# Hybrid decoder trunk, one core: the second product's first weights loaded ahead of two weight blocks, one PSUM bank changed, table steps and convolution taps put elsewhere

## The chip, the cores and the metric

The kernel runs on one core of one Trainium2 chip. Times are device microseconds (us) of a whole execution; "before" is the median of three runs. The trace is one further execution, taken by the hardware profiler. Engine names are the profile's: PE is TensorE's matmul, PEld its weight load, DVE is VectorE, ACT is ScalarE, POOL is GpSimd, SP is SyncE, which here only issues DMAs.

## The reference, cut to what matters

A sequence of 512 tokens of width 1024, all in float32, goes through two layers. The first is a recurrent layer, the second an attention layer, and each ends in a SwiGLU unit with 2816 hidden columns.

```python
def causal_depthwise_conv(x, w, b):            # 4 taps per channel
    y = lax.conv_general_dilated(x, w[:, None, :], ..., feature_group_count=x.shape[-1])
    return y + b

def recurrent_mixer(h, w_in, conv_w, conv_b, ga_w, ga_b, gx_w, gx_b, lam, w_out):
    y_branch, x_branch = jnp.split(h @ w_in, 2, axis=-1)
    gate = jax.nn.gelu(y_branch, approximate=True)
    xc = causal_depthwise_conv(x_branch, conv_w, conv_b)
    return (gate * rg_lru(xc, ga_w, ga_b, gx_w, gx_b, lam)) @ w_out

def swiglu(h, w_in, w_out):
    g, u = jnp.split(h @ w_in, 2, axis=-1)
    return (jax.nn.silu(g) * u) @ w_out

h = h + recurrent_mixer(rms_norm(h, ...), ...);          h = h + swiglu(rms_norm(h, ...), ...)   # layer 1
h = h + dilated_attention_mixer(rms_norm(h, ...), ...);  h = h + swiglu(rms_norm(h, ...), ...)   # layer 2
```

`rg_lru` multiplies blocks of 128 channels of the convolved branch with two gate matrices. The attention uses tables of cosines and sines of the positions (rotary embedding).

## The kernel before, in words

**Matmuls.** Every float32 product is made of three matmuls over a high part (h) and a low part (l) of each operand: `mm3`, lines 163 to 165. So each weight piece that arrives raw by DMA has to be split first: ACT casts it to the high part (L117, or L656 for the SwiGLU's first product), and DVE subtracts that from the raw piece to get the low part (L124, L657). A piece is 128 x 1024. The class `Stream` loads raw pieces into two buffers named wr, by SP's DMA queue, and splits them into three pairs named wh and wl.

**Order.** In most of the program a scheduler orders the instructions of each engine by dependencies and priorities. Inside a SwiGLU (`swiglu`), DVE, ACT, SP, POOL and PE run in exactly the order in which the code is written. SP takes its DMAs in that order too, and an issue that waits holds up all behind it.

**The recurrent layer's projection** goes over 16 blocks of 128 output columns; the first eight are the x branch. For each block `x_block` evicts the PSUM bank with a DVE multiply into xp (L443 for block 4, at high priority; L445 for the others), makes the first tap of the convolution on ACT (blocks 0 to 3, L449) or POOL (blocks 4 to 7, L451), and the other three taps on DVE (L453). `x_parts` splits the result into xch and xcl (L279, L280), and `x_gates` multiplies these with the gate matrices; its second product of each block uses the two banks tagged PT, one of which block 4 of the projection holds at first.

**A SwiGLU** starts with four plain blocks (`plain_block`, weights wr). Then the hidden columns go in five groups q = 0 to 4 (`ORDERS`), each as seven products named GA, GB, S1 to S4 and UB, which share operands in the manner of Strassen and Winograd: S1 and S3 are sums of weight blocks, made by a plain DMA on SP and an accumulating DMA on POOL (`fetch`, L640 and L642). "O" in the list is an out block, a part of the second product (`out_block`); in group 0 it makes four outputs b = 0 to 3, evicted by L776 into the residual h, in later groups two, evicted by L774. "L" splits the operands of the next out blocks (`parts_of`, L729 and L730).

```python
MIDDLE = "S1.T1 GA.B11 GB.B21 L S2.T2 O O S3.T3 O S4.B22 O UB.T4"
ORDERS = ["GA.B11 GB.B21 O S1.T1 S2.T2 O S3.T3 S4.B22 UB.T4", MIDDLE, MIDDLE, MIDDLE,
          "S1.T1 GA.B11 GB.B21 L S2.T2 O S3.T3 S4.B22 UB.T4 O O L O"]
```

So the step numbers s are 0 to 3 for the plain blocks and 4 to 12 for group 0; the first out block is step 6, between GB and S1. Each product has two outputs in two banks. GA uses the two banks PT; GB uses X and one of the three mm; S1 uses O and S. After GB, DVE adds its two banks to GA's result (`gate`, L700), which frees X and the mm bank; the plain blocks and the out blocks take mm banks in turn, and the out block's third output (b = 2) takes S in step 6 and X in step 9.

**Tables.** The rotary tables (`rotary`, L875 to L929, small DVE operations and two Sin activations) are a generator. The first SwiGLU advances it by one `yield` after step 9 and after each step from 13 on.

**Attention** stands between the two SwiGLUs and isn't touched.

Of the kernel before, what the change touches and what calls it, by code (L numbers as in the profile page):

```python
# [20 lines left out]
ALU = mybir.AluOpType  # L21
# [3 lines left out]
T = 512  # L25
# [28 lines left out]
def behind(tc, inst, f):  # L54

    tc.add_manual_dep(inst.ins, f.ins.name, mybir.DependencyInfo(
        mybir.DependencyClass.NoSync, mybir.DependencyReason.DATA), reason="order")
# [99 lines left out]
def trunk(tc, A, out):  # L157
    nc = tc.nc
    V, S, G, PE = nc.vector, nc.scalar, nc.gpsimd, nc.tensor

    def mm3(ps, w, x, first, last, on=False):
        (wh, wl), (xh, xl) = w, x
        PE.matmul(ps, wh, xh, start=first, stop=False, skip_group_check=on)  # L163
        PE.matmul(ps, wh, xl, start=False, stop=False, skip_group_check=on)  # L164
        PE.matmul(ps, wl, xh, start=False, stop=last, skip_group_check=on)  # L165
# [55 lines left out]
    with tc.tile_pool(name="keep", bufs=1) as kp, tc.tile_pool(name="wts", bufs=3) as wp, \  # L221
# [6 lines left out]
        def bank(tag=None, name="ps"):  # L228
            tag = tag or next(rotation)
            return pp.tile([128, 512], F32, name=name, tag=tag, bufs={"mm": 3, "PT": 2}.get(tag, 1))  # L230
# [42 lines left out]
        def split(src, gain, hi, lo):  # L273
            a = S.activation(hi, src, AF.Copy, scale=gain)  # L274
            V.scalar_tensor_tensor(lo, src, gain, hi.bitcast(F32), ALU.mult, ALU.subtract)
            return a
# [13 lines left out]
        def gain(c, k):  # L290
            return par[:, c + k:c + k + 1]
# [46 lines left out]
        with tc.tile_pool(name="lru", bufs=2) as lp, \  # L338
# [32 lines left out]
            for k in range(KB):  # L371
                with tc.high_priority():
                    a = split(h[k], gain(C_AN, k), xh[k], xl[k])
# [5 lines left out]
            def in_block(i, tag=None, between=None, at=5):  # L379
                ps = bank(tag)  # L380
                wh, wl = ws.get(i)
                for k in range(KB):
                    c = slice(128 * k, 128 * k + 128)
                    mm3(ps, (wh[:, c], wl[:, c]), (xh[k], xl[k]), k == 0, k == KB - 1)
                    if k == at and between:
                        between()
                return ps

            parts = [ws.get(0), ws.get(1)]
            first = [bank(), bank()]  # L390
# [15 lines left out]
            rb = norm[1]  # L406
# [10 lines left out]
            def perm(t):  # L417
                return t.rearrange("q (n i p) -> q n p i", n=4, i=32, p=4)

            def mine(t):  # L420
                return t.rearrange("q (n p i) -> q n p i", n=4, p=4, i=32)
# [16 lines left out]
            def x_block(b, ps):  # L438
                xp = lp.tile([128, 640], F32, name="xp", bufs=2)[:, :T + 4]
                G.memset(xp[:, 0:3], 0.0)  # L440
                if b == 4:
                    with tc.high_priority():
                        V.tensor_tensor(perm(xp[:, 3:3 + T]), mine(ps), mine(rb), ALU.mult)  # L443
                else:
                    V.tensor_tensor(perm(xp[:, 3:3 + T]), mine(ps), mine(rb), ALU.mult)  # L445
                xc = lp.tile([128, T], F32, name="xc", bufs=5)
                cw = [par[:, C_CW + 4 * b + j:C_CW + 4 * b + j + 1] for j in range(4)]
                if b < 4:
                    S.activation(xc, xp[:, 0:T], AF.Identity, bias=gain(C_CB, b), scale=cw[0])  # L449
                else:  # L450
                    G.tensor_scalar(xc, xp[:, 0:T], cw[0], gain(C_CB, b), ALU.mult, ALU.add)  # L451
                for j in range(1, 4):
                    V.scalar_tensor_tensor(xc, xp[:, j:j + T], cw[j], xc, ALU.mult, ALU.add)  # L453
                return b, xc

            def x_parts(b, xc):
# [50 lines left out]
                hgl[b] = lp.tile([128, T], F32R, name="hgl", tag=f"gated{b}", bufs=1)  # L507
                halve(z, hgh[b], hgl[b])

            xs, ys, decayed, ready = [], [], [], 0  # L510
            ws.asp = 2
            for i, m in enumerate(lru_order):
                ps = first.pop(0) if first else in_block(p_in + i)

                if i in (5, 6, 8, 9):
                    for _ in range(2):
                        b = xs[0][0]
# [23 lines left out]
            for ms in ((0, 1), *((m,) for m in range(2, 8))):  # L541
                parts = [ws.get(p_aout + m) for m in ms]
                first = [bank() for m in ms]
# [8 lines left out]
        def by_time(t):  # L552
            return t.rearrange("q (t a i) -> q a t i", t=4, a=4)

        def in_turn(t):
            return t.rearrange("q (a t i) -> q a t i", t=4, a=4)
# [11 lines left out]
        def swiglu(fp, p, after, meanwhile=iter(())):  # L568
# [64 lines left out]
            def fetch(q, n):  # L633
                if q == len(ORDERS):
                    return
                r = raws[q, n] = fp.tile([128, 4, 512], F32, name=n, bufs=1)
                u, k = {"GA": (0, 0), "GB": (0, 1), "S1": (1, 0), "S3": (0, 0), "UB": (1, 1)}[n]
                for i in range(2):
                    c = r[:, 2 * i:2 * i + 2]
                    nc.sync.dma_start(c, p.part(u, q, k, i))  # L640
                    if n in ("S1", "S3"):
                        nc.gpsimd.dma_start(c, p.part(1, q, n == "S1", i), accum_op=ALU.add)  # L642
# [120 lines left out]
            def out_block(c, m, i):  # L763
                nb = 2 if c else 4
                wh, wl = (t.rearrange("q (b k m) -> q b k m", b=nb, m=128) for t in ws.get(i))
                nk = 8 // nb
                src = [x if c else x[:, 2:4] for x in chunks[c]]
                for b in range(nb):
                    ps = bank("mm" if b != 2 else "X" if m else "S")
                    for k in range(nk):  # L770
                        mm3(ps, (wh[:, b, k], wl[:, b, k]), [x[:, k] for x in src], k == 0, k == nk - 1)
                    x = h[m + b]
                    if c:
                        V.tensor_tensor(by_time(x), by_time(x), in_turn(ps), ALU.subtract)  # L774
                    else:
                        V.tensor_tensor(x, x, ps, ALU.subtract)  # L776
# [4 lines left out]
            with tc.manual_schedule(engines={E.PE, E.DVE, E.Activation, E.SP, E.Pool}):  # L781
                ws.load_to(p.steps[2][3])
                fetch(0, "GA")
                ws.load_to(p.steps[3][3])
                for n in ("GB", "S1", "S3", "UB"):
                    fetch(0, n)
                for s, (kind, *what) in enumerate(p.steps):
                    if kind == "product" and what[0] == len(ORDERS) - 1:
                        ws.al = 4
                    {"plain": plain_block, "product": product, "out": out_block, "parts": parts_of}[kind](*what)  # L790
                    early.get(s, lambda: None)()
                    if s == 9 or s > 12:
                        next(meanwhile, None)
                for _ in meanwhile:
                    pass
# [13 lines left out]
        with tc.tile_pool(name="tables", bufs=1) as rp:  # L809
            rp = Pool(rp)  # L810
            with tc.tile_pool(name="ffn1", bufs=2) as fp:
                fp = Pool(fp)
                tables = []

                def make_tables():
                    tables.extend((yield from rotary(nc, A, rp, fp)))

                def after_f1(m, ps):
                    V.tensor_tensor(by_time(h[m]), by_time(h[m]), in_turn(ps), ALU.subtract)
                    split(h[m], gain(C_KV, m), xh[m], xl[m])  # L820
                    squares(m, Temps(fp))

                swiglu(fp, p_f1, after_f1, make_tables())


            with tc.tile_pool(name="att", bufs=2) as ap:
                ap = Pool(ap)
                attention(tc, A, ap, ws, dict(locals()))

        with tc.tile_pool(name="ffn2", bufs=2) as fp:  # L830
            fp = Pool(fp)

            def after_f2(m, ps):

                halves = [(slice(0, 2), nc.scalar), (slice(2, 4), nc.sync)]
                for c, queue in halves if m == 7 else [(slice(0, 4), nc.sync)]:
                    x = by_time(h[m])[:, :, c]
                    V.tensor_tensor(x, x, in_turn(ps)[:, :, c], ALU.subtract)
                    c = slice(128 * c.start, 128 * c.stop)
                    queue.dma_start(out[m][:, c], h[m][:, c])  # L840

            swiglu(fp, p_f2, after_f2)
# [532 lines left out]
```

## Time and profile before

| | |
|---|---|
| median of three runs | 1179.7 us (1177.21 to 1182.56) |
| the profiled execution | 1177.11 us |
| its span, from the first to the last instruction | 1175.1 us |
| granted TensorE clock | 1.00 throughout |
| PE busy | 1153.3 us, 98% of the span |
| DVE busy | 852.3 us, 73% |
| ACT busy | 623.3 us, 53% |
| POOL busy | 189.1 us, 16% |
| moved by DMA | 179.61 MB, mean 153 GB/s |
| first SwiGLU, first matmul of group 0's GA | 175.5 us of the span |
| second SwiGLU, last matmul of group 0's GB | 861.1 us |

A row of the order of time gives the start in us, the duration in us, the engine, the line, the operation, the tiles (out<-in; buffer numbers left out, so S stands for S1 and S3, wr for all raw buffers), the shapes, how many instructions of the kind are merged in it (x4), and in brackets how long the engine stood idle before it and whose end let it go. A row of waits gives the total in us, the number of waits and the longest. TensorE's matmuls overlap: one lasts 0.39 us but the next starts 0.23 us after it.

### The profile page before, as it was taken

What the parts mean: (1) busy time and instruction counts of PE and PEld (TensorE: products, weight loads), DVE (VectorE), ACT (ScalarE), POOL (GpSimd) and SP (SyncE); (2) the same over time, 40 slices, a digit from 0 to 9 for tenths busy, and PEclk for the clock granted to TensorE, in tenths of its full rate; (3) what the DMA queues carried; (4) which work ended last, traced back from release to release, by engine and by line L of the source; (5) the groups of instructions that cost most, each with busy time, mean ns of one, the idle gap of its engine ahead of it and who ended that gap; (6) DMA issues with size and microseconds to landing.
All of it is one profiled execution on the core that took longest, in us unless ns stands there. A gap on an engine that the chain in (4) does not pass through costs nothing.

```text
span 1175.1 us, 15129 instructions
## 1 busy us (share of the span) xinstructions
PE 1153.3 (98%) x5403; PEld 951.6 (81%) x5403; DVE 852.3 (73%) x1525; ACT 623.3 (53%) x901; POOL 189.1 (16%) x221
## 2 busy tenths in 40 slices
PE   9999999999999999999999999999989999999998
PEld 6787887878888888888888888898868888888887
DVE  8988687877767676887564677765968767676764
ACT  6796455543535353665555677655545535353532
POOL 4210010201001000010511334341101101001000
PEclk9999999999999999999999999999999999999999
DMA  7643365965665722433988658435648675757324
GB/s 238 155 112 108 108 225 151 236 182 162 182 170 166 193 73 81 132 101 99 222 178 179 136 120 178 108 73 126 227 115 231 182 177 165 193 160 181 89 65 133
DMA packets 92234, 179.61 MB, mean 153 GB/s; under 512 B 8704, under 2 KB 27008, under 8 KB 92160
## 3 DMA queue, kind: packets, MB, share of 16 engines
q1 hardware_dynamic: 72720, 130.80, 34.7%
q0 software_dynamic: 18864, 47.19, 22.8%
q8 instruction: 43, 0.70, 0.3%
q10 hardware_dynamic: 576, 0.66, 0.2%
q14 instruction: 31, 0.25, 0.1%
HBM read 164.99 MB, written 2.10 MB: 142 GB/s over the span
## 4 chain that ended last, share of the span: by engine, by line
PE 82%; DVE 6%; DMA 4%; issue 3%; ACT 2%; POOL 1%; SPq 0%; ACTq 0%; DVEq 0%; POOLq 0%
PE ps L165 22%; PE ps L164 22%; PE ps L163 21%; PE ps L1038 5%; PE ps L1039 5%; PE ps L1040 5%; DMA wr<-in_f_out 2%; DVE xc L453 1%; PE ps L1117 1%; PE ps L1204 1%; DMA wl<-in_w_in 1%; DMA GB<-in_f_in 1%; ACT pr L1190 0%; DMA h<-in_x 0%; DVE xp L445 0%
## 5 line engine op out<-in xcount | busy, mean ns | idle before, releaser
L117 ACT CAST wh<-wr 128x1024 fp32r<-128x1024 f32 (+2 forms) x136 | 131.1, 969 | 141.3 <-PE ps L164 80.9
L164 PE MATMUL ps<-wl,xh 128*128 128x512 f32 x320 | 124.6, 389 | 0.0
L165 PE MATMUL ps<-wh,xl 128*128 128x512 f32 x320 | 124.6, 389 | 0.0
L163 PE MATMUL ps<-wh,xh 128*128 128x512 f32 x320 | 124.6, 389 | 0.0
L165 PE MATMUL ps<-gh,wl 128*128 128x512 f32 x288 | 114.7, 398 | 1.9 <-DVE wl L124 1.7
L124 DVE TENSOR_TENSOR wl<-wr,wh 128x1024 fp32r<-128x1024 f32 (+2 forms) x93 | 100.0, 1084 | 21.9 <-ACT wh L117 21.5
L163 PE MATMUL ps<-gh,wh 128*128 128x512 f32 x288 | 113.8, 395 | 1.7 <-ACT wh L117 1.7
L164 PE MATMUL ps<-gl,wh 128*128 128x512 f32 x288 | 113.6, 395 | 0.0
L642 POOL DMA_DIRECT2D S<-in_f_in x40 | 48.2, 1248 | 380.9 <-DMA S<-in_f_in 241.3
L656 ACT CAST wh<-S 128x1024 fp32r<-128x1024 f32 x60 | 63.0, 1050 | 76.1 <-PE ps L165 33.8
L163 PE MATMUL ps<-xh,wh 128*128 128x512 f32 x256 | 101.0, 396 | 0.6 <-ACT xh L274 0.6
L165 PE MATMUL ps<-xh,wl 128*128 128x512 f32 x256 | 100.0, 391 | 0.7 <-DMA wl<-in_w_in 0.7
L164 PE MATMUL ps<-xl,wh 128*128 128x512 f32 x256 | 100.2, 391 | 0.1
L163 PE MATMUL ps<-wh,T 128*128 128x512 f32 x240 | 93.8, 391 | 5.4 <-DVE h L776 5.4
L657 DVE TENSOR_TENSOR wl<-S,wh 128x1024 fp32r<-128x1024 f32 x60 | 73.2, 1223 | 33.6 <-ACT wh L656 33.6
L165 PE MATMUL ps<-wh,T 128*128 128x512 f32 x240 | 93.5, 390 | 0.0
L164 PE MATMUL ps<-wl,T 128*128 128x512 f32 x240 | 93.5, 389 | 0.0
L1038 PE MATMUL ps<-wh,xh 128*128 128x512 f32 x224 | 91.5, 408 | 0.0
L1040 PE MATMUL ps<-wh,xl 128*128 128x512 f32 x224 | 87.7, 392 | 0.0
L1039 PE MATMUL ps<-wl,xh 128*128 128x512 f32 x224 | 87.4, 390 | 0.0
L774 DVE TENSOR_TENSOR h<-h,ps 128x512 f32<-128x512 f32 x64 | 43.4, 686 | 55.6 <-PE ps L165 55.4
L163 PEld LDWEIGHTS ps<-wh,xh 128*128 128x128 f32 x320 | 60.1, 188 | 12.7
(285 smaller groups left out, 2673.5 us busy)
## 6 DMA issues: line engine op xcount, KB each, us to landing
S<-in_f_in SPq DMA_DIRECT2D x40, 512.0 KB, 6.4
S<-in_f_in POOLq DMA_DIRECT2D x40, 512.0 KB, 8.9
wr<-in_f_out SPq DMA_DIRECT2D x36, 512.0 KB, 5.3
wr<-in_w_q SPq DMA_DIRECT2D x28, 512.0 KB, 6.8
wl<-in_w_q POOLq DMA_DIRECT2D x28, 512.0 KB, 7.6
GA<-in_f_in SPq DMA_DIRECT2D x20, 512.0 KB, 4.8
GB<-in_f_in SPq DMA_DIRECT2D x20, 512.0 KB, 7.5
UB<-in_f_in SPq DMA_DIRECT2D x20, 512.0 KB, 5.6
```

The lines of the kernel that those rows point to most:

```text
L117: nc.scalar.copy(hi[:, c], r[:, c])
L124: a = eng.tensor_tensor(lo[:, c], r[:, c], hi[:, c].bitcast(F32), ALU.subtract)
L163: PE.matmul(ps, wh, xh, start=first, stop=False, skip_group_check=on)
L164: PE.matmul(ps, wh, xl, start=False, stop=False, skip_group_check=on)
L165: PE.matmul(ps, wl, xh, start=False, stop=last, skip_group_check=on)
L642: nc.gpsimd.dma_start(c, p.part(1, q, n == "S1", i), accum_op=ALU.add)
L656: S.copy(hi, r)
L657: V.tensor_tensor(lo, r, hi.bitcast(F32), ALU.subtract)
L774: V.tensor_tensor(by_time(x), by_time(x), in_turn(ps), ALU.subtract)
L1038: PE.matmul(ps[t], xh[k][:, r], wh[:, c], start=k == 0, stop=False)
L1039: PE.matmul(ps[t], xh[k][:, r], wl[:, c], start=False, stop=False)
L1040: PE.matmul(ps[t], xl[k][:, r], wh[:, c], start=False, stop=k == 7)
```

## The change: what it does

There are four edits, in `x_block` and in `swiglu`.

1. **Weights of the second product.** The transfers of S3 and UB for group 0 are issued after step 0 instead of before it. The raw weights of the first out block are requested within step 0, so on SP's queue they now stand ahead of S3 and UB. This holds for both SwiGLUs.
2. **A bank.** The third output of the first out block (step 6, m = 0, b = 2) takes bank X instead of S.
3. **The tables' steps.** After step 12 the generator is advanced only after out blocks and after the products S3 and S4.
4. **The convolution.** Block 3's three DVE taps are put off until block 4's bank has been evicted, and the first of them is ordered behind that eviction; block 4's eviction loses its high priority.

```diff
-                if b == 4:
-                    with tc.high_priority():
-                        V.tensor_tensor(perm(xp[:, 3:3 + T]), mine(ps), mine(rb), ALU.mult)
-                else:
-                    V.tensor_tensor(perm(xp[:, 3:3 + T]), mine(ps), mine(rb), ALU.mult)
+                out_of_bank = V.tensor_tensor(perm(xp[:, 3:3 + T]), mine(ps), mine(rb), ALU.mult)
...
-                for j in range(1, 4):
-                    V.scalar_tensor_tensor(xc, xp[:, j:j + T], cw[j], xc, ALU.mult, ALU.add)
+
+                def taps(first=None):
+                    for j in range(1, 4):
+                        a = V.scalar_tensor_tensor(xc, xp[:, j:j + T], cw[j], xc, ALU.mult, ALU.add)
+                        if first and j == 1:
+                            behind(tc, a, first)
+
+                if b == 4:
+                    put_off.pop()(out_of_bank)
+                if b == 3:
+                    put_off.append(taps)
+                else:
+                    taps()
                 return b, xc
...
-                    ps = bank("mm" if b != 2 else "X" if m else "S")
+                    ps = bank("X" if b == 2 else "mm")
...
-                for n in ("GB", "S1", "S3", "UB"):
+                for n in ("GB", "S1"):
                     fetch(0, n)
...
                     early.get(s, lambda: None)()
-                    if s == 9 or s > 12:
+                    if s == 0:
+                        fetch(0, "S3")
+                        fetch(0, "UB")
+                    if s == 9 or s > 12 and (kind == "out" or kind == "product" and what[1][:2] in ("S3", "S4")):
                         next(meanwhile, None)
```

The bank changes no engine's order, only what an instruction waits for. The other edits move instructions at these places.

SP's queue at the start of the second SwiGLU before; wr175 is the fourth plain block's piece, wr180 and wr185 are the weights of the two out blocks of group 0:

```order
L640 DMA GA_7595<-in_f2_in 128x2x512 x2
L100 DMA wr175_7598<-in_f2_in 128x1024
L640 DMA GB_7600<-in_f2_in 128x2x512 x2
L640 DMA S1_7603<-in_f2_in 128x2x512 x2
L640 DMA S3_7608<-in_f2_in 128x2x512 x2
L640 DMA UB_7613<-in_f2_in 128x2x512 x2
L93 DMA wr180_7617<-in_f2_out 128x4x256
L93 DMA wr185_7810<-in_f2_out 128x4x256
```

and with the change (lines 640 and 642 are now 647 and 649):

```order
L647 DMA GA_7595<-in_f2_in 128x2x512 x2
L100 DMA wr175_7598<-in_f2_in 128x1024
L647 DMA GB_7600<-in_f2_in 128x2x512 x2
L647 DMA S1_7603<-in_f2_in 128x2x512 x2
L93 DMA wr180_7609<-in_f2_out 128x4x256
L647 DMA S3_7682<-in_f2_in 128x2x512 x2
L647 DMA UB_7687<-in_f2_in 128x2x512 x2
L93 DMA wr185_7810<-in_f2_out 128x4x256
```

The first out block's weights have moved ahead of S3's and UB's four transfers; the rest stands as before.

DVE in the convolution before, from the evictions of blocks 2 and 3 on; xp_432 and xc_435 belong to block 2, xp_440 and xc_443 to block 3, xp_456 and xc_459 to block 4, xp_528 to block 5:

```order
L445 TENSOR_TENSOR xp_432<-ps_262,rb_345 128x4x4x32
L445 TENSOR_TENSOR xp_440<-ps_310,rb_345 128x4x4x32
L453 SCALAR_TENSOR_TENSOR xc_435<-xp_432,par_74,xc_435 128x512
L453 SCALAR_TENSOR_TENSOR xc_443<-xp_440,par_74,xc_443 128x512
L453 SCALAR_TENSOR_TENSOR xc_435<-xp_432,par_74,xc_435 128x512
L453 SCALAR_TENSOR_TENSOR xc_443<-xp_440,par_74,xc_443 128x512
L453 SCALAR_TENSOR_TENSOR xc_435<-xp_432,par_74,xc_435 128x512
L453 SCALAR_TENSOR_TENSOR xc_443<-xp_440,par_74,xc_443 128x512
L443 TENSOR_TENSOR xp_456<-ps_356,rb_345 128x4x4x32
L445 TENSOR_TENSOR xp_528<-ps_464,rb_345 128x4x4x32
L280 TENSOR_TENSOR xcl_537<-xc_435,xch_536 128x512
L453 SCALAR_TENSOR_TENSOR xc_459<-xp_456,par_74,xc_459 128x512
```

and with the change (L441 is the eviction of every block, L451 the taps on DVE; block 4's tiles are now xp_453 and xc_456, and xcl_541 is block 3's low part):

```order
L441 TENSOR_TENSOR xp_440<-ps_310,rb_345 128x4x4x32
L451 SCALAR_TENSOR_TENSOR xc_435<-xp_432,par_74,xc_435 128x512 x3
L441 TENSOR_TENSOR xp_453<-ps_356,rb_345 128x4x4x32
L451 SCALAR_TENSOR_TENSOR xc_443<-xp_440,par_74,xc_443 128x512
L280 TENSOR_TENSOR xcl_537<-xc_435,xch_536 128x512
L451 SCALAR_TENSOR_TENSOR xc_443<-xp_440,par_74,xc_443 128x512
L451 SCALAR_TENSOR_TENSOR xc_456<-xp_453,par_74,xc_456 128x512
L451 SCALAR_TENSOR_TENSOR xc_443<-xp_440,par_74,xc_443 128x512
L451 SCALAR_TENSOR_TENSOR xc_456<-xp_453,par_74,xc_456 128x512
L483 TENSOR_TENSOR gated0_408<-ig_511,xc_419 128x512
L280 TENSOR_TENSOR xcl_541<-xc_443,xch_540 128x512
```

Block 4's eviction now stands behind three taps instead of six, block 5's has moved to a later place, and block 3's low part stands behind two taps of block 4. On PE the gate product that takes over block 4's bank stands eight matmuls of the projection earlier than before.

DVE in group 1 of the first SwiGLU before; L700 is the gate after GB, L730 the operands of the out blocks, wl52 and wl53 the low parts of their weights:

```order
L700 TENSOR_TENSOR e_2089<-ps_2093,e_2089 128x512
L875 TENSOR_SCALAR grow_1855<-grow_1855 128x384
L876 CAST posf_1861<-pos_1857 128x8
L877 TENSOR_TENSOR rtmp_1864<-posf_1861,inv_1859 128x128
L882 TENSOR_SCALAR rtmp_1864<-rtmp_1864 128x128
L883 TENSOR_SCALAR rtmp_1864<-rtmp_1864 128x128
L886 SCALAR_TENSOR_TENSOR rtmp_1864<-rtmp_1864 128x128
L730 TENSOR_TENSOR gl_1985<-gl_1985,gh_1984 128x512 x4
L882 TENSOR_SCALAR rtmp_1864<-rtmp_1864 128x128
L883 TENSOR_SCALAR rtmp_1864<-rtmp_1864 128x128
L886 SCALAR_TENSOR_TENSOR rtmp_1864<-rtmp_1864 128x128
L124 TENSOR_TENSOR wl52_2150<-wr52_1962,wh52_2149 128x1024
```

and with the change, where the six operations now stand; L760 evicts S3, wl57 and wl58 are the low parts of S4's two halves:

```order
L664 TENSOR_TENSOR wl57_2261<-GB_1885,wh57_2260 128x1024
L760 TENSOR_TENSOR e_2043<-ps_2046,e_2043 128x512
L760 TENSOR_TENSOR e_2043<-ps_2047,e_2043 128x512
L885 TENSOR_SCALAR grow_1855<-grow_1855 128x384
L886 CAST posf_1861<-pos_1857 128x8
L887 TENSOR_TENSOR rtmp_1864<-posf_1861,inv_1859 128x128
L892 TENSOR_SCALAR rtmp_1864<-rtmp_1864 128x128
L893 TENSOR_SCALAR rtmp_1864<-rtmp_1864 128x128
L896 SCALAR_TENSOR_TENSOR rtmp_1864<-rtmp_1864 128x128
L664 TENSOR_TENSOR wl58_2285<-GB_1885,wh58_2284 128x1024
```

The nine operations are gone from between the gate and the out blocks' weights; six of them stand between S3's evictions and the second half of S4's weights, the next three behind the following out block.

More of the change, by code (lines that the diff above doesn't have):

```diff
@@ L508, in y_gate @@
                 halve(z, hgh[b], hgl[b])
-            xs, ys, decayed, ready = [], [], [], 0
+            xs, ys, decayed, ready, put_off = [], [], [], 0, []
             ws.asp = 2
```

## The prediction

> **What bounds the kernel now.** I read the page first, then the waits of TensorE, then the order of time at each wait. The page:
>
> ```profile
> span 1175.1 us, 15129 instructions
> PE 1153.3 (98%) x5403; PEld 951.6 (81%) x5403; DVE 852.3 (73%) x1525; ACT 623.3 (53%) x901; POOL 189.1 (16%) x221
> ```
>
> TensorE is the bound: it stands still for 1175.1 - 1153.3 = 21.8 us, and no matmul is removed, so the change can only win part of those. The waits of TensorE (us in total, times, longest) say which:
>
> ```profile
> PE ps L163 <- DVE h L776: 5.4, 2, 3.5
> PE ps L165 <- DVE wl L124: 1.7, 2, 1.2
> PE ps L163 <- ACT wh L117: 1.7, 1, 1.7
> ...
> PE ps L163 <- DVE xp L443: 1.0, 1, 1.0
> ```
>
> 9.8 us on four releasers, and the change touches each. L776 evicts the first out block (the unit m=0 of group 0), L117 and L124 split its weights, L443 evicts convolution block 4. I price each wait from start to start, against the even pitch of 0.23 us between matmuls; a restart costs about 0.1 us more (the next matmul follows after 0.33 instead of 0.23).
>
> **Weights of the first out block, and its banks, in the second SwiGLU.** In order of time (start, us, engine, what it waited for):
>
> ```profile
> 861.10 0.39 PE L165 MATMUL ps<-wh,xl 128*128 128x512 f32 x1
> 862.05 1.04 ACT L117 CAST wh<-wr 128x1024 fp32r<-128x1024 f32 x1 [4.43 <-DMA wr<-in_f_out]
> ...
> 863.15 0.50 PE L163 MATMUL ps<-gh,wh 128*128 128x512 f32 x1 [1.66 <-ACT wh L117]
> ...
> 863.48 0.39 PE L164 MATMUL ps<-gl,wh 128*128 128x512 f32 x1
> ...
> 864.41 0.50 PE L165 MATMUL ps<-gh,wl 128*128 128x512 f32 x1 [0.54 <-DVE wl L124]
> ...
> 870.11 0.40 PE L165 MATMUL ps<-wh,T 128*128 128x512 f32 x1
> ...
> 874.03 0.51 PE L163 MATMUL ps<-wh,T 128*128 128x512 f32 x1 [3.52 <-DVE h L776]
> ```
>
> The cast stands idle 4.43 us for a DMA. TensorE loses 863.15 - 861.10 - 0.23 = 1.82 on the high part, 864.41 - 863.48 - 0.23 = 0.70 on the low part and two restarts: **2.7 us**. At 874.03 the first matmul of S1 into bank S waits for the eviction L776, because the out block's third output (b=2) was put in S: 874.03 - 870.11 - 0.23 = 3.69 and a restart: **3.8 us**.
>
> Why the DMA was late: the SP queue, and the landing times (median us from issue; the second row is the transfer issued at 834.91, the first of S3's two).
>
> ```profile
> 833.79 2.04 SPq L640 DMA_DIRECT2D S<-in_f_in  x4
> 836.45 2.92 SPq L640 DMA_DIRECT2D UB<-in_f_in  x2
> 839.81 4.72 SPq L93 DMA_DIRECT2D wr<-in_f_out  x2
> ```
>
> ```profile
> wr<-in_f_out SPq DMA_DIRECT2D x2, 512.0 KB, 22.5
> S<-in_f_in SPq DMA_DIRECT2D x1, 512.0 KB, 11.7
> ```
>
> The change puts these weights where S3's first transfer was: four 512 KB transfers (S3, UB) now stand behind them. They should land about when that transfer did, 834.91 + 11.7 = 846.6, instead of near 862. The cast then has its place after the cast that ended at 862.05 - 4.43 = 857.6, so the whole 4.43 us goes with 11 us to spare. The load waits for a raw-weight buffer that the third plain block frees; nothing in SP's rows stops there before 834.9, so I put that wait at nothing. What stands behind it on SP are S3 and UB, one transfer later each, and POOL's accumulating DMA for S3 follows by as much; S3's use is far off (below, the last rival).
>
> With the weights there, what is late next? The first SwiGLU shows it, since there they came just in time:
>
> ```profile
> 186.38 0.40 PE L163 MATMUL ps<-gh,wh 128*128 128x512 f32 x1
> ...
> 187.38 1.28 DVE L700 TENSOR_TENSOR e<-ps,e 128x512 f32<-128x512 f32 x2
> ...
> 189.17 0.40 PE L163 MATMUL ps<-gh,wh 128*128 128x512 f32 x1
> ...
> 192.44 0.40 PE L165 MATMUL ps<-wh,T 128*128 128x512 f32 x1
> ...
> 194.74 0.50 PE L163 MATMUL ps<-wh,T 128*128 128x512 f32 x1 [1.90 <-DVE h L776]
> ...
> 195.19 1.22 DVE L657 TENSOR_TENSOR wl<-S,wh 128x1024 fp32r<-128x1024 f32 x1
> ```
>
> The out block starts at 186.38 without a wait, and only bank S is late: 194.74 - 192.44 - 0.23 = 2.07 and a restart, **2.2 us**. Output b=2 starts 12 matmuls in, at 189.17, and will now go into bank X. X holds GB's first half until the first of the two adds at L700 has read it: 187.38 + 0.64 = 188.0. It is free 1.1 us early, so this costs nothing; the add hides it, and each us that the add slips over 1.1 comes back as a wait. Bank S is then free long before S1. After S1 the next need is S2's first low part, at L657 behind the four evictions: 195.19 + 1.22 = 196.4. S1's third matmul of 24 is at 192.44, so S2 begins 22 matmuls later, at 197.5, and this holds by 1 us too. The second SwiGLU should now repeat the first one's timing. So 2.7 + 3.8 + 2.2 = 8.7 us.
>
> **The tables' steps.** In the first SwiGLU's group 1, six small DVE operations, and later three more, stand between the gate and the split of the out block's weights (the rows are the first and last of the six, the TensorE matmuls on both sides, and the same place one group later):
>
> ```profile
> 244.24 0.35 DVE L875 TENSOR_SCALAR grow<-grow 128x384 f32<-128x384 f32 x1
> ...
> 245.55 0.29 DVE L886 SCALAR_TENSOR_TENSOR rtmp<-rtmp 128x128 f32<-128x128 f32 x1
> ...
> 249.01 0.40 PE L164 MATMUL ps<-gl,wh 128*128 128x512 f32 x1
> ...
> 250.57 0.50 PE L165 MATMUL ps<-gh,wl 128*128 128x512 f32 x1 [1.16 <-DVE wl L124]
> ```
>
> ```profile
> 310.94 0.40 PE L164 MATMUL ps<-gl,wh 128*128 128x512 f32 x1
> 311.36 0.50 PE L165 MATMUL ps<-gh,wl 128*128 128x512 f32 x1
> ```
>
> TensorE loses 250.57 - 249.01 - 0.23 = 1.33 and a restart, 1.4. Without the steps the place still loses what the later group loses: 311.36 - 310.94 - 0.23 = 0.19 and a restart, 0.3. Gain **1.1 us**. The six now come behind S3's evictions, ahead of S4's second low part; from 244.24 to the end of the last they take 1.6 us. S4's second half is needed 12 matmuls (2.8 us) into S4, and an out block of 24 matmuls (5.6 us) lies between S3 and S4, so I price the new place at nothing; at worst the 1.1 comes back. The two Sin activations and the remaining steps finish one group later, far ahead of attention.
>
> **The convolution.** Before, taps of blocks 2 and 3 alternate ahead of the eviction that frees the bank for a gate product:
>
> ```profile
> 41.49 0.75 DVE L453 SCALAR_TENSOR_TENSOR xc<-xp,par,xc 128x512 f32<-128x512 f32 x1
> 42.41 3.40 DVE L453 SCALAR_TENSOR_TENSOR xc<-xp,par,xc 128x512 f32<-128x512 f32 x5 [0.17 <-ACT xc L449]
> 45.73 1.08 DVE L443 TENSOR_TENSOR xp<-ps,rb 128x512 f32<-128x512 f32 x1
> ...
> 46.95 0.47 PE L163 MATMUL ps<-xch,gwh 128*128 128x512 f32 x1 [1.02 <-DVE xp L443]
> ```
>
> ```profile
> 44.57 0.86 POOL L121 DMA_DIRECT2D wl<-in_w_in  x1 [7.13 <-ACT wl L120]
> ```
>
> ```profile
> L451 POOL TENSOR_SCALAR xc<-xp,par x4: 761/1788/2828, 47.0 to 61.7; 128x512 f32<-128x512 f32 x4
> ```
>
> ```profile
> 98.25 0.50 PE L165 MATMUL ps<-xh,wl 128*128 128x512 f32 x1 [0.70 <-DMA wl<-in_w_in]
> ```
>
> That product waits about 1.2 from start to start, so its place was 45.75. Now block 2's three taps (0.67 each, 3.40 / 5) end at 43.5, the eviction at 44.6, and the product can start at 44.7. But it also moved ahead of eight matmuls, so its place is 45.75 - 8 x 0.23 = 43.9, and it still waits some 0.8: the gain there is 0.4, not 1.2. Behind it DVE meets block 4's first tap, which waits for POOL's operation (L451; shortest, median and longest in ns above). POOL can start that at 45.5, behind the DMA issue at 44.57, and ends it by the median at 47.3. Five DVE instructions at 0.67 then end with block 3's low part at 50.6. TensorE needs that 31 matmuls after the product, at 44.7 + 31 x 0.23 = 51.8. And what is won at 44.7 can be lost at 98.25, where TensorE waits for an accumulating DMA that hangs on ACT's queue, not on TensorE. I take **0.3 us**, between -0.6 (2.83 us on POOL: the low part comes at 51.7, just in time, but ACT's casts and the DMA at the end come 1.0 later than by the median, against 0.4 won) and +1.3 (the whole wait and its restart).
>
> [...]
>
> **Sum.** 8.7 + 1.1 + 0.3 = 10.1 us. The profiled execution took 1177.11 us (2.0 outside the span) and would take 1167.0, with a span of 1165.0. The median of the three runs, 1179.7, lies 2.6 above it; the forecast on it is 1169.6.
>
> **Rivals.**
> *The weights still land late* in the second SwiGLU, the change not doing there what it says. The two waits at 863.15 and 864.41 stay, and b=2 meets bank X before the late add has read it (some 0.6), so 2.7 + 0.6 are lost: gain 6.8, 1172.9 us. For it: SP's transfers come slower once POOL's accumulating ones run (22.5 us from issue to landing against 11.7 five us earlier in the queue). Against: the slot's own landing at 846.6, which had the first of them beside it. 0.09. [...]
> *POOL holds DVE up in the convolution:* at 2.83 us the term falls to -0.6 and, if the gate products of blocks 2 and 3 slip as well, to -1.5; gain 8.3 to 9.2, near 1171. For it the longest row; against, that TensorE needs the low part 1.2 us after my estimate. 0.12.
> *A wait takes the place of the one removed:* S2's low parts or bank X come late because DVE, 73% busy, has lost the pause that the stall gave it. Decides from a slip of 1 us in either SwiGLU; at 2.5 us of slip 1.5 us are lost in each: gain 7, 1172.7. 0.08.
> *Slower: S3's weights starve.* They now stand behind the out block's load; if that load waits for its buffer, S3, UB and POOL's accumulation stand still.
>
> ```profile
> S<-in_f_in POOLq DMA_DIRECT2D x1, 512.0 KB, 14.5
> ```
>
> ```profile
> 848.27 1.19 POOL L642 DMA_DIRECT2D S<-in_f_in  x1 [0.16 <-issue]
> ...
> 881.84 1.05 ACT L656 CAST wh<-S 128x1024 fp32r<-128x1024 f32 x1 [1.19 <-PE ps L165]
> ```
>
> The last accumulation, issued at 848.27, lands at 862.8; S3's cast at 881.84 moves 6.5 earlier, to 875.3. From 12.5 us of delay it costs, once in each SwiGLU; 21 us of delay would cost 17 and give 1186.6. 0.03.
>
> **How the numbers follow.** Forecast 0.68, the rivals 0.09, 0.12, 0.08 and 0.03. A measurement of this kernel can tell about 0.5% (5.9 us) from no change, and the three runs lie 5.4 us apart. The range: at the good end all bounds, 8.7 + 1.4 + 1.3 = 11.4, and 2.3 for the scatter of a median, 1166.0; at the other the first and third rival, 1172.9, and 1.6 of scatter, 1174.5. The first three rivals are still faster by more than 5.9 us, but two of them by about 1 us only, so a part of them and of the scatter goes to "same": faster 0.86, same 0.11, slower 0.03.
>
> **What would show it.** Right: no TensorE wait on the eviction of the first out block (now L783) in either SwiGLU, the weights' DMA landing some 11 to 12 us after its issue and the cast beside GB's matmuls, no wait above 0.3 us on the out block's low part in group 1, span near 1165. Wrong: a wait of TensorE on L707 (bank X) or on S2's low part, on the convolution's low part near 51 us, a longer wait at 98 us, or ACT waiting for S3's DMA.

## The result, and the profile after

The changed kernel takes 1166.66 us (median of 6 runs, 1165.99 to 1168.45) against 1179.78 us before (6 runs, 1177.21 to 1182.56): 13.1 us less, a ratio of 0.9892, 95% interval 0.9876 to 0.9908. In later groups of runs the kernel before took 2981.67 and 1928.67 us once each; medians, ranges and ratios leave these two runs out. The forecast was 1169.6 us, between 1166.0 and 1174.5. The profiled execution of the changed kernel took 1166.22 us. First the page:

```profile
span 1164.4 us, 15128 instructions
PE 1151.9 (99%) x5403; PEld 952.2 (82%) x5403; DVE 851.5 (73%) x1525; ACT 623.8 (54%) x901; POOL 186.3 (16%) x221
```

TensorE now stands still for 1164.4 - 1151.9 = 12.5 us instead of 21.8, and its busy time has hardly moved. The waits of TensorE (us in total, times, longest), with the first five of the list:

```profile
PE ps L346 <- DVE warm L343: 1.4, 1, 1.4
PE ps L1127 <- ACT qt L1129: 1.3, 2, 1.0
PE ps L165 <- DVE ql L280: 1.3, 2, 0.7
PE ps L163 <- ACT qt L1129: 1.2, 1, 1.2
PE ps L163 <- DVE xp L441: 1.0, 1, 1.0
```

Of the four rows shown before three are gone: the evictions of the first out block (now L783), and the high and the low part of its weights. The fifth row is the fourth of them, the convolution's gate product, and it is as long as it was. What stays besides is the kernel's start and attention, which the change doesn't touch.

The second SwiGLU in order of time, first ACT, then DVE, then TensorE. These rows answer to the ones around 861 to 874 us before:

```profile
852.46 1.05 ACT L279 CAST gh<-w 128x1024 fp32r<-128x1024 f32 x1
853.41 1.05 ACT L117 CAST wh<-wr 128x1024 fp32r<-128x1024 f32 x1
```

```profile
858.23 1.28 DVE L707 TENSOR_TENSOR e<-ps,e 128x512 f32<-128x512 f32 x2
...
863.65 2.47 DVE L783 TENSOR_TENSOR h<-h,ps 128x512 f32<-128x512 f32 x4
866.04 1.22 DVE L664 TENSOR_TENSOR wl<-S,wh 128x1024 fp32r<-128x1024 f32 x1
```

```profile
856.99 0.39 PE L165 MATMUL ps<-wh,xl 128*128 128x512 f32 x1
857.22 0.40 PE L163 MATMUL ps<-gh,wh 128*128 128x512 f32 x1
...
860.01 0.40 PE L163 MATMUL ps<-gh,wh 128*128 128x512 f32 x1
...
862.58 0.39 PE L165 MATMUL ps<-gh,wl 128*128 128x512 f32 x1
862.81 0.39 PE L163 MATMUL ps<-wh,T 128*128 128x512 f32 x1
...
863.27 0.39 PE L165 MATMUL ps<-wh,T 128*128 128x512 f32 x1
863.51 0.39 PE L163 MATMUL ps<-wh,T 128*128 128x512 f32 x1
...
868.26 0.39 PE L163 MATMUL ps<-wh,T 128*128 128x512 f32 x1
```

The cast of the weights at 853.41 has no idle time in front of it and no DMA behind it, and TensorE goes into the out block (857.22) and out of it into S1 (862.81) at the even pitch of 0.23. S1's fourth matmul is its first into bank S, and at 863.51 it follows the third after 0.24. Bank X is free at 858.23 + 0.64 = 858.87, and the third output needs it at 860.01. S2's first low part ends at 867.26, and S2 begins at 868.26. Both margins are the 1 us that was forecast. The weights' DMA (KB, us from issue to landing), issued at 830.76:

```profile
wr<-in_f_out SPq DMA_DIRECT2D x1, 512.0 KB, 11.8
```

It took 22.2 us before, when it stood behind S3 and UB. The cast has 853.41 - 842.57 = 10.8 us to spare.

S1's third and fourth matmul in the first SwiGLU, where the fourth came 2.07 us late before:

```profile
191.73 0.39 PE L165 MATMUL ps<-wh,T 128*128 128x512 f32 x1
191.96 0.39 PE L163 MATMUL ps<-wh,T 128*128 128x512 f32 x1
```

The low part in the first SwiGLU's group 1, and the convolution (first TensorE, then DVE):

```profile
246.08 0.40 PE L164 MATMUL ps<-gl,wh 128*128 128x512 f32 x1
246.51 0.50 PE L165 MATMUL ps<-gh,wl 128*128 128x512 f32 x1
```

```profile
45.46 0.47 PE L163 MATMUL ps<-xch,gwh 128*128 128x512 f32 x1 [0.95 <-DVE xp L441]
```

```profile
39.87 1.97 DVE L441 TENSOR_TENSOR xp<-ps,rb 128x512 f32<-128x512 f32 x2
41.87 2.33 DVE L451 SCALAR_TENSOR_TENSOR xc<-xp,par,xc 128x512 f32<-128x512 f32 x3
44.24 1.08 DVE L441 TENSOR_TENSOR xp<-ps,rb 128x512 f32<-128x512 f32 x1
```

The group's wait has fallen to the 0.2 that every later group has. The gate product still waits: 1.12 us from start to start beyond the pitch, against 1.18 before.

One thing doesn't fit yet. The spans of the two profiled executions differ by 10.7 us, the medians by 13.1. The profiled execution of before lay 2.7 us below the median of its kernel, that of after only 0.4 below. The forecast had carried the 2.6 us over as a fixed distance. The experiments had to find what they are.

### The profile page after: what moved, and what is told of

It reads as the page before. It is cut to its first block, busy times and chain, and to the rows that moved or that the text cites. A ratio compares the mean times of both kernels' runs of the same rounds, so it can differ in the third digit from the quotient of the medians.

```text
span 1164.4 us, 15128 instructions
## 1 busy us (share of the span) xinstructions
PE 1151.9 (99%) x5403; PEld 952.2 (82%) x5403; DVE 851.5 (73%) x1525; ACT 623.8 (54%) x901; POOL 186.3 (16%) x221
## 4 chain that ended last, share of the span: by engine, by line
PE 92%; DVE 3%; ACT 2%; issue 1%; DMA 1%; POOL 0%; ACTq 0%; DVEq 0%; SPq 0%
PE ps L165 25%; PE ps L164 25%; PE ps L163 25%; PE ps L1048 5%; PE ps L1049 5%; PE ps L1050 5%; PE ps L1127 1%; PE ps L1214 1%; DVE xc L451 1%; DMA h<-in_x 0%; ACT pr L1200 0%; PE ps L296 0%; DVE ql L280 0%; ACT wh L117 0%; DMA wr<-in_w_in 0%
```

## The experiments

Times of one group were measured on one chip, beside runs of the kernel before there. "Lost" means here: from one matmul's start to the next's, less 0.228 us.

**One part of the change at a time.** Each kernel is the kernel before with one part (before: 1178.67 us, 23 runs).

The order of the DMAs:

```diff
-                for n in ("GB", "S1", "S3", "UB"):
+                for n in ("GB", "S1"):
...
+                    if s == 0:
+                        fetch(0, "S3")
+                        fetch(0, "UB")
```

> The kernel before with one part of the change alone: the DMAs of S3 and UB of the first block are issued after the first loop step, so the first out block's weights stand ahead of them. Theory (four separable losses): in the second SwiGLU both weight waits go (2.7 us) and the wait of S1 for bank S shrinks from 3.8 us to the first SwiGLU's 2.2 us; the first SwiGLU and the tables' wait stay. Gain in span 4.3 us. If the wider scatter of the kernel before comes from these late weights, the times of this kernel lie closer together (2.5 us instead of 5.4) and its median gains up to 2.4 us more, 6.7. Rival (the weights still land late): the landing is above 20 us after the issue, the waits stay, gain below 1 us. Rival (S3 starves): an ACT wait for a DMA at S3's cast.

Measured: 1172.07 us (1171.78 to 1173.18, 5 runs), ratio 0.9947 (0.9934 to 0.9959), so 6.6 us by the medians, and the runs lie 1.4 us apart. The waits of TensorE:

```profile
PE ps L163 <- DVE h L776: 3.8, 2, 1.9
```

Both waits for weights are gone, and the wait for bank S is now 1.9 in both SwiGLUs. The theory holds, with the larger of its two gains.

The bank of the third output:

```diff
-                    ps = bank("mm" if b != 2 else "X" if m else "S")
+                    ps = bank("X" if b == 2 else "mm")
```

> The kernel before with the bank of the first unit's third output alone changed (X instead of S). Theory: both waits of S1 for bank S go, 2.2 us in the first SwiGLU and 3.8 us in the second; the late weights' 2.7 us stay. Gain in span 6.0 us, or 5.4 if the late add of the gate still holds bank X for 0.6 us in the second SwiGLU. Rival (a wait takes the place of the one removed): a TensorE wait of 1 us or more on the add that reads bank X, or on S2's low part, in either SwiGLU, gain 4 us or less. If the late weights cause the scatter of the kernel before, this kernel scatters as widely as that one.

Measured: 1170.60 us (1169.31 to 1173.35, 5 runs), ratio 0.9939 (0.9927 to 0.9952): 8.1 us, more than forecast. The two parts alone add up to 14.7 us, more than the whole change's 13.1: the wait for bank S in the second SwiGLU shrinks with either of them. No wait on an out block's eviction is left, and a short one on bank X has come:

```profile
PE ps L165 <- DVE wl L124: 1.2, 1, 1.2
...
PE ps L163 <- DVE e L700: 0.4, 1, 0.4
```

The first row is the tables' wait in group 1, which stays here. The second is the rival's mechanism, at the price given for it: the add of the gate holds bank X, and TensorE loses 0.57 us. In this execution the late weights landed 19.6 us after their issue instead of 22.2, and the high part cost nothing. This execution took 1169.31 us and was the fastest of the five, which lie 4.0 us apart.

The tables' steps, and the convolution's taps (in the second kernel the taps alone are as in the change):

```diff
-                    if s == 9 or s > 12:
+                    if s == 9 or s > 12 and (kind == "out" or kind == "product" and what[1][:2] in ("S3", "S4")):
```

> The kernel before with the tables' steps alone moved to S3's and S4's products and out blocks. Theory: the wait on the out block's low part in group 1 falls from 1.4 us to 0.3 us, nothing else changes: gain in span 1.1 us, which the times can hardly tell from nothing, so the trace decides. Rival: the steps at their new place hold up S4's second low part and the 1.1 us come back there: gain 0.

> The kernel before with the convolution's taps alone moved behind the eviction of block 4. After the changed kernel's profile: the wait at the gate product hardly changes (0.06 us less), and what is in question is the wait of 0.97 us at 98 us for an accumulating DMA, which was gone there. Theory 1 (the wait at 98 us comes and goes with the DMA's own time, 6.6 to 7.9 us): gain 0.1 us, and the wait at 98 us may be there or not, with the landing following the transfer's time and not its issue. Theory 2 (the new order brings that DMA forward): the wait at 98 us is gone, issue or landing earlier by 0.7 us or more, gain 1.0 us.

Measured: 1178.90 us (12 runs), ratio 0.9999 (0.9989 to 1.0010), and 1180.71 us (12 runs), ratio 1.0011 (1.0000 to 1.0022). The trace of the first shows the wait gone, as the theory has it:

```profile
251.52 0.40 PE L164 MATMUL ps<-gl,wh 128*128 128x512 f32 x1
251.95 0.50 PE L165 MATMUL ps<-gh,wl 128*128 128x512 f32 x1
```

That is 0.3 us with its restart, instead of 1.4. But the times don't show the 1.1 us, since the runs of this kernel lie 6.0 us apart. The convolution's kernel is not faster. Its gate product still loses 1.12 us. Its DMA took 6.9 us to land and there was no wait at 98 us, but the kernel with the new DMA order, whose convolution is the old one, had none either (6.4 us).

**The kernel before once more, profiled.**

> The kernel before, profiled once more. Theory (a stretch of 3.41 us in which TensorE stands still for 1.86 us or more is followed by one of 3.41 us at half clock, and the stretches run on a clock of their own, so that it depends on the execution which waits trigger it): at least one stretch at half clock in the second SwiGLU behind the waits at 863 or 874 us, each with 6 to 8 matmuls at a pitch of 0.43 us and 1.2 to 1.6 us lost; span 1176 to 1180 us. Rival (only the times of DMAs vary): no stretch at half clock, and a longer span shows as longer waits for DMAs.

Measured: 1180.24 us, span 1178.3, 3.2 longer than the first profile's. Two pairs of windows (PE, PEld, DVE, ACT and POOL busy, then the granted clock):

```profile
192.75:196.16 3.41, 0.00 (x0) 0.00 (x0) 3.38 (x6) 0.12 (x1) 0.00 (x0) 1.00 0.17 35
196.16:199.57 3.41, 3.38 (x8) 2.70 (x9) 2.84 (x3) 0.00 (x0) 0.00 (x0) 0.50 0.72 273
865.17:868.59 3.42, 1.67 (x6) 1.11 (x7) 2.22 (x2) 2.00 (x2) 0.00 (x0) 1.00 0.03 11
868.59:872.00 3.41, 3.41 (x10) 2.62 (x9) 2.56 (x4) 1.37 (x3) 0.00 (x0) 0.50 0.00 0
```

In each pair TensorE has little to do in the first stretch of 3.41 us, and the clock is halved (0.50) in the second. There a matmul follows the last after 0.43 us, as these rows of TensorE show:

```profile
196.19 0.79 PE L163 MATMUL ps<-wh,T 128*128 128x512 f32 x1 [3.53 <-DVE h L776]
196.78 0.63 PE L164 MATMUL ps<-wl,T 128*128 128x512 f32 x1
197.21 0.63 PE L165 MATMUL ps<-wh,T 128*128 128x512 f32 x1
```

The same execution has a longer wait for bank S in the first SwiGLU: 3.53 instead of 1.90. The weights there landed 20.4 us after their issue, in the first profile 17.9:

```profile
wr<-in_f_out SPq DMA_DIRECT2D x1, 512.0 KB, 20.4
```

So both theories had a part of it: half clock, and DMAs of another length. In the first SwiGLU the two go together over the traces with the old order and the old bank: landing 17.9, 18.9, 19.7 and 20.4 us after the issue, bank S lost 2.07, 2.78, 3.70 and 3.70 us. The way from one to the other goes through DVE, which splits the block's weights, adds the gate and then evicts, in this order: in the second profile the split of these weights ended at 186.52 us and the third eviction at 196.14, in the first at 185.06 and 194.68, so both are 1.5 us later. What TensorE lost in all around the first out block of each SwiGLU (120 to 200 and 840 to 885 us of the span), summed from its starts:

```
                                 first SwiGLU   second SwiGLU
before                               2.3             6.5
before, again                        6.1             6.8
tables' steps alone                  4.4             9.6
convolution alone                    4.1             8.3
mean of these four                   4.2             7.8
DMA order alone                      3.9             2.2
bank alone                           0.3             0.9
the change                           0.1             0.0
```

Two of the four are kernels that differ from the one before only elsewhere. The execution on which the prediction was made is the luckiest of the four in both places. The clocks of the 23 runs say the same. The first profile's mean granted clock is 1.000, the second's, with its two stretches at half clock, 0.997. Of the 23 runs 18 have 0.997 or less, with a median of 1179.45 us; the other five, with 0.998 to 1.000, have one of 1177.17. With the new DMA order alone all five runs have 0.998 or more.

**Six long pauses against eighteen short ones.** Both kernels are the changed one with 36 added matmuls in groups 1 to 3 of each SwiGLU; the results of these aren't used. In one, six copies by ACT in a row hold TensorE up once in a group; in the other two copies do so three times. The core of the edit, with n = 6 behind S3 and 0 elsewhere, or n = 2 behind each of the three:

```diff
+                    if kind == "product" and what[0] in (1, 2, 3) and what[1][:2] in ("GA", "S3", "UB"):
...
+                            PE.matmul(ps, xh[0][:, :128], xh[0], start=True, stop=True)
+                            for j in range(n):
+                                S.copy(z, last.bitcast(F32) if j else ps)
+                                last = z
...
+                            PE.matmul(ps, xh[0][:, :128], z, start=True, stop=True)
```

> The changed kernel with six long pauses of TensorE: in groups 1 to 3 of both SwiGLUs, behind the product S3, a matmul that waits for six copies by ACT in a row; 36 added matmuls in all, at three places of each group (the results of these aren't used). Theory (half clock behind idle time): each pause of about 3.9 us leaves at least 1.95 us idle in one stretch of 3.41 us, so each of the six is followed by a stretch at half clock and loses 1.2 to 1.6 us more: 8.2 (matmuls) + 23.4 (pauses) + 8.5 = 40 us over the changed kernel. Rival (only the pause itself is lost): 32 us over it.

> The same 36 added matmuls, but the copies by ACT spread: two copies at each of the three places of a group, behind the products GA, S3 and UB, so 18 pauses of about 1.5 us. Theory and rival alike: no stretch holds 1.86 us of idle time, so no half clock: 8.2 (matmuls) + 27 (pauses) + 1.8 (restarts) = 37 us over the changed kernel. What tells the theories apart is the comparison: by the theory the six long pauses cost 3 us more than these 18 though TensorE stands still for 4 us less; by the rival they cost 5 us less.

Measured: 1209.53 us (4 runs) with the long pauses and 1206.06 us (4 runs) with the short ones, so 3.5 us more where the rival had 5 us less. Over the changed kernel's 1166.4 us (on another chip) that is 43 and 40 us, some 3 us more than forecast in both; only a part of these 3 us is accounted for. The pauses themselves lost 6 x 4.08 = 24.5 us in the one and 28.3 us in the other, 1.1 and 1.3 us more than forecast. All six long ones are followed by half clock; one of them:

```profile
958.97:962.38 3.41, 0.30 (x1) 0.30 (x2) 0.00 (x0) 3.28 (x6) 0.00 (x0) 1.00 1.12 205
962.38:965.79 3.41, 3.41 (x9) 2.65 (x8) 1.22 (x1) 0.59 (x1) 0.00 (x0) 0.50 0.84 160
```

Two of the six bring two such stretches in a row, which the expectation hadn't. The kernel with short pauses has none between its start and its end. The rival falls.

**The convolution in the changed kernel, and the waits that are left.** Four kernels side by side (before: 1179.55 us, 10 runs). The changed kernel itself:

> The changed kernel again, as the measure for the three kernels beside it. Both theories: 1166.7 us, its runs closer together than those of the kernel before (2.5 us against 5.4 us), no stretch at half clock behind the first 10 us.

Measured: 1166.36 us (1165.88 to 1168.06, 6 runs), no half clock between the start and the end.

With the convolution's taps as they were:

```diff
-                if b == 4:
-                    put_off.pop()(out_of_bank)
-                if b == 3:
-                    put_off.append(taps)
-                else:
-                    taps()
+                for j in range(1, 4):
+                    V.scalar_tensor_tensor(xc, xp[:, j:j + T], cw[j], xc, ALU.mult, ALU.add)
```

> The changed kernel with the convolution's taps as before. Theory (the edit is worth 0.1 us at the gate product, and the wait at 98 us follows the DMA's own time): median within 0.5 us of the changed kernel's; the wait at 98 us is there when the accumulating DMA takes over 7 us from issue to landing, and not otherwise. Rival 1 (the edit brings the DMA forward): about 1.0 us slower than the changed kernel. Rival 2 (the edit costs, since the kernel before with it alone came out 1.3 us slower, between 0 and 2.6): about 1 us faster than the changed kernel.

Measured: 1167.81 us (1166.06 to 1169.13, 6 runs), ratio 0.9902 (0.9879 to 0.9925) against 0.9894 (0.9872 to 0.9916): 1.4 us slower by the medians, inside both intervals, and of the other sign than the edit alone had. This execution has the wait at 98 us, with a DMA of 7.9 us:

```profile
98.63 0.50 PE L165 MATMUL ps<-xh,wl 128*128 128x512 f32 x1 [0.74 <-DMA wl<-in_w_in]
```

With the low parts last in the first block of an out block:

```diff
+                        for k in range(nk):
+                            for x in src:
+                                PE.matmul(ps, wh[:, b, k], x[:, k], start=x is src[0] and k == 0, stop=False)
+                        for k in range(nk):
+                            PE.matmul(ps, wl[:, b, k], src[0][:, k], start=False, stop=k == nk - 1)
```

> The changed kernel with the first block of each out block multiplied in another order: all products with the weights' high part first, those with the low part after them. Theory: the eight waits of 0.2 us on the low part, each with a restart of 0.1 us, go: 2.4 us faster than the changed kernel, some 1164.3 us. Rival (what is late moves on to the next instruction on the same engine): the wait reappears within the next twelve matmuls, gain below 0.5 us.

Measured: 1164.27 us (1163.48 to 1165.60, 6 runs), ratio 0.9875 (0.9851 to 0.9899), 2.1 us under the changed kernel beside it. All eight waits are gone, and none came in their place; span 1162.6 against 1165.0. This kernel has the changed convolution, and the wait at 98 us all the same, with a DMA of 8.1 us:

```profile
98.08 0.50 PE L165 MATMUL ps<-xh,wl 128*128 128x512 f32 x1 [0.76 <-DMA wl<-in_w_in]
```

That settles the wait at 98 us for kernels whose TensorE comes to it at about the same time. There are thirteen traces in this study. In the twelve besides that of the kernel below, the wait is there in the six in which the DMA took 7.6 to 8.1 us, and in none of the six in which it took 6.4 to 7.1, and both kinds are found with the old convolution and with the new one.

With the gate product later as well:

```diff
-                for g, ps in enumerate((pr, pi)):
-                    mm3(ps, (gwh[g][:, c], gwl[g][:, c]), parts, True, True)
+                mm3(pr, (gwh[0][:, c], gwl[0][:, c]), parts, True, True)
...
+                ps = first.pop(0) if first else in_block(p_in + i, None, late.pop() if late else None, 2)
```

> The kernel with the low parts last, and the second gate product of convolution block 1 issued some 6 matmuls later, so that the eviction of block 4 is done by then. Theory: the wait of 1.2 us on that eviction goes as well: 1.2 us faster than the kernel with the low parts last, some 1163.1 us. Rival (the gates' chain becomes late instead): a wait of about the same length near 51 us on block 3's low part or at a later bank, no gain.

Measured: 1164.13 us (1163.25 to 1164.64, 5 runs), ratio 0.9872 (0.9849 to 0.9896). The gate product is where it should be and waits for nothing:

```profile
45.61 0.39 PE L165 MATMUL ps<-xh,wl 128*128 128x512 f32 x1
45.84 0.39 PE L163 MATMUL ps<-xch,gwh 128*128 128x512 f32 x1
```

By the medians 0.1 us is left of the 1.2: the forecast missed, though the wait itself went. What is won here makes TensorE earlier at the DMA of 98 us, which it doesn't move, and there a part of it is lost again even in this execution, whose DMA took only 6.4 us. It landed at 96.91, and the matmul that needs it started at 96.95:

```profile
96.43 0.39 PE L164 MATMUL ps<-xl,wh 128*128 128x512 f32 x1
96.95 0.50 PE L165 MATMUL ps<-xh,wl 128*128 128x512 f32 x1
```

That is 0.29 us and a restart, 0.4 in all, where no other trace with a DMA that short has a wait. A DMA of 8 us, 1.6 later, would take the rest of the 1.2 as well; this is worked out from these rows and no run shows it. All runs of this kernel and of the one before it are faster than all of the changed kernel's; the two can't be told apart.

## Why the prediction was right, and where it was off

**Weights of the first out block, 2.7 us.** Right in every step: place, landing (11.7 forecast, 11.8 measured), 11 us to spare (10.8), no wait on SP for the raw-weight buffer. S3 and UB behind it starved nobody.

**The banks, 3.8 and 2.2 us.** Right in mechanism, and the two margins of 1 us were met. The sizes are right for that one execution, and too small for the kernel: these are the terms that were mis-sized. The four traces lose 12.0 us around the first out blocks on average (4.2 + 7.8), not 8.7. With the 1.1 us of the tables' steps that makes 13.1, as much as the medians differ, though a mean over four executions can't be as exact as that. Two things make the rest, and both hang on waits that the change removes. The weights land by up to 2.5 us later than in the first profile of the first SwiGLU ("there they came just in time" was true of that execution alone), and the wait for bank S grows from 2.07 to 3.70 us. And some waits are followed by half clock, 6 to 8 matmuls at 0.2 us more each, so 1.2 to 1.6 us.

The failed step is therefore in the sum: "the median of the three runs, 1179.7, lies 2.6 above it; the forecast on it is 1169.6". The 2.6 us were taken for scatter that stays. They were part of the loss, and went with it; the forecast came out 2.9 us high. The runs show it too: those of before lie 5.0 us apart (23 runs), those with the new DMA order alone 1.4 (5 runs), those of the changed kernel 2.5 (6 runs).

**Half clock ahead of a longer wait.** When a stretch at half clock is followed by a longer wait for another engine, it can cost nothing. In the second profile of before, bank S in the second SwiGLU lost 2.14 us instead of 3.69: from the start of the out block on TensorE came there 1.5 us later, and DVE, which it waits for, did not. The trace of the convolution alone has the same, with 2.16.

**The tables' steps, 1.1 us.** Right, by the traces of the part alone and of the whole; nothing came back at the new place. The times of the part alone are too wide apart to show it.

**The convolution, 0.3 us.** The forecast had 0.4 us won at the gate product, and 0.06 was. It put the three taps of block 2 at 0.67 us each, as they ran when two blocks alternated. In the new order each tap stands right behind the one whose result it needs, and three took 2.33 us, 0.78 each: this is the step that was mis-sized, by 0.3 us. The taps also started 0.4 us later, but so did TensorE's work there. So the eviction ended at 45.3 instead of 44.6, and the product waited for about as long as before at an earlier place. POOL's first tap there (45.55 us) took 1.56 us, and the tap that DVE started beside it (46.40 us) took 1.25 where the next three took 0.74. The forecast's lower end, a loss of 0.6, isn't shown by any run: TensorE met its low part without a wait, and the edit changes no time that can be measured.

**The rivals.** The late landing, S2's low parts, a starved S3 and a longer wait at 98 us didn't come. The wait on bank X came where it was put, in the kernel that has the bank without the DMA order, and cost 0.57 us (0.6 forecast): the order of the DMAs is what makes the bank's part free.

## What to carry to other kernels

A single profiled execution prices a wait at what it was that time: look at how far the runs lie apart, and at whether the wait hangs on a DMA, before its length is taken for a constant. TensorE's idle time can cost twice, once as the wait and once as a slow clock behind it, so several short waits can be better than one long one of the same sum: here six pauses that lost 24.5 us made a kernel 3.5 us slower than eighteen that lost 28.3. Where a gain moves the engine closer to a transfer that doesn't move, count only what is left behind that transfer.

## What the hardware showed that was not expected

**Half clock behind a wait.** In all thirteen traces the clock, once it is up, changes only at the borders of stretches of 3.41 us, which follow on one another and lie elsewhere in each execution: borders at 192.75, 196.16 and, 197 stretches on, 868.59 us in the second profile of before, at 190.49 and 193.91 with the DMA order alone. Taking 0.228 us for each matmul, the 13 stretches at full clock in which TensorE worked 1.32 us or less were all followed by one at half clock; of the other 4372, from 1.36 us upward (the kernel's start and end left out), none was. The expectation had put the bound at 1.86 us of idle time, from the ends of matmuls, which the profile only models; counted by starts it is sharper. Here are two that just escaped, in the first profile of before, with a wait of 3.52 us between them (1.36 us of work in the first):

```profile
868.94:872.36 3.42, 1.56 (x7) 0.94 (x5) 2.63 (x3) 1.76 (x2) 0.00 (x0) 1.00 0.00 0
872.36:875.77 3.41, 1.74 (x8) 1.45 (x9) 3.41 (x6) 0.00 (x0) 0.00 (x0) 1.00 0.66 226
```

The wait was cut in two by the border. A wait of 2.09 us that lay inside one stretch (up to 193.50 us, DMA order alone, 1.32 us of work in the stretch) was enough for half clock:

```profile
190.49:193.91 3.42, 1.50 (x7) 0.93 (x6) 3.42 (x5) 1.05 (x1) 0.00 (x0) 1.00 0.25 73
193.91:197.32 3.41, 3.41 (x10) 2.64 (x9) 2.40 (x3) 0.00 (x0) 0.00 (x0) 0.50 0.62 234
```

The shorter wait was enough, and the longer one, cut in two, was not.

**Dependent operations on DVE.** The convolution's tap, a 128x512 operation that lasts 0.75 us by itself (41.49 us, before), came every 0.67 us where the taps of two blocks alternated (before, five in 3.40 us from 42.41 us on) and every 0.78 us where each needed the one right before it (the changed kernel, three in 2.33 us from 41.87 us on).
